# A one-core Hymba decoder step: token sums as one job ahead of the key tiles, other job times, another quarter order in the last tile, and more raw weight buffers in the gate stage

## The chip, the cores and the metric

The kernel runs on one core of one Trainium2 chip. The metric is the device time of one execution in microseconds (us), lower is better. For the kernel before, three timed runs gave a median of 2141.79 us (2141.38 to 2145.74).

The core has a matrix engine (PE, its weight loads listed as PEld), a vector engine (DVE), a scalar engine (ACT), a general engine (POOL) and an engine that mainly issues DMA transfers (SP). Each works through its own instruction stream in program order. A scheduler in the build decides that order, unless a `pin` or a `with tc.high_priority()` in the code says otherwise, and it puts in the semaphore waits.

## What is computed

The reference is one decoder layer for a prompt of 1024 tokens and 8 single-token samples with a paged cache of 4096 positions each. Width is 2048, everything is fp32.

```python
p = project(rmsnorm(xp, norm_w), w_in, b_igate, b_fgate)     # one input projection, split by columns
att = dsa_prompt(q, k, v, qi, ki, wi)    # indexer scores, top-256 positions per token, attention on those
h_ml, C1, n1, m1 = mlstm_run(mq, mk, mv, ig, lf, ...)        # mLSTM recurrence in chunks of 64
xp = merge(xp, att, p, h_ml, ml_norm_w, w_out)               # gates (az, mo, mz), output projection, residual
s = project(rmsnorm(xs, norm_w), ...)                        # the same for the 8 samples
att_s = dsa_sample(...)                  # indexer scores against the cached index keys, top 256, attention
h_s, C2, n2, m2 = mlstm_run(...)         # one recurrent step from the given state
xs = merge(xs, att_s, s, h_s, ml_norm_w, w_out)
y_prompt, y_sample = rmsnorm(xp, final_norm_w), rmsnorm(xs, final_norm_w)
```

Returned are y, the new keys, values and index keys, and the recurrent states, for the prompt and the samples.

## The kernel before

**Products.** An fp32 operand is split into a rounded part H and a remainder L, and a product is three matmuls, H·H, H·L and L·H, summed in PSUM. A weight block arrives by a DMA into a raw buffer (`wraw`); ACT rounds it into `wH` (line 251) and DVE subtracts to get `wL` (line 252). The tokens x (1032 columns: 1024 of the prompt, 8 samples) stand in SBUF as 16 rows of 128, each as xH and xL.

**Stages.** The main line of the program is PE work in six parts, by the span of the profiled run: tiles 0 to 8 of the input projection, each 128 columns wide and read in four weight quarters (misc columns, then the index queries; evacuated by DVE line 377 into `iqe`), to about 178 us; the value stage (`vproj`, lines 1559 and 1564), to 428 us; twenty tiles 17 to 36 with attention keys, values, queries and mLSTM queries and keys (line 1490), to 968 us; the gate stage (line 1717), to 1780 us; the samples' part of the output projection (line 1926), to 1882 us; the output product (line 1987), to the end.

**The gate stage** computes three gates for 24 pairs of 128 columns by a seven-product scheme of the Strassen kind: sums of weight blocks (`usD`) and sums of token blocks (`xsD`) are made beforehand in DRAM, and then 84 products (`product`) of 48 matmuls each run, with partial results added up by DVE line 1797 into buffers of a ring called `outs`. Each product takes a 128x2x512 weight block through a raw buffer, ACT line 1707 and DVE line 1708. The first two products use the tile stage's rings; from the third on there are two raw buffers, `wraw` and `wH`, and the rounded and remainder parts go into `halves`, which are the unused upper columns of the x rows 8 to 15.

**Jobs.** All else runs beside this as jobs in three lanes. A job is a generator that emits a few instructions and yields a weight; after each quarter of a tile, or at the corresponding moments of the other stages, `Lane.step` lets each lane emit as much as its job needs to be done by its `end`, counted in tiles: `T_MV` is 9 (value stage), `T_AK` 17 (first key tile), `T_MQ` 29, `T_G` 37 (gate stage), `T_PRE` 58. In the gate stage a product counts as 0.29 tiles. Lane 0 runs gates, index, att and ml; lane 1 runs prep, dscore, prep2, dsel, datt and dml; lane 2 runs usum. Those that the change touches:

- **prep** and **prep2** make the token sums for four of the eight row pairs k each. Per k: two loads X on SP (line 1386), two 1032-wide DVE operations (1391), four sums on POOL (1394 to 1397), and ten `hl` steps: an ACT rounding (1378), a DVE subtraction (1379) and an SP store to `xsD` (1380), through three buffers.
- **dscore** scores the samples against the cached index keys in 32 chunks: POOL gathers a chunk into `kp` (line 994, three buffers, two chunks ahead), PE multiplies it (line 1014).
- **usum** makes the weight sums: SP copies a block to `usD` (line 1408) and POOL adds another to it by an accumulating DMA (line 1409), 48 of these.
- **index**, **dsel** are the top-256 searches of prompt and samples (lines 489 to 566 and 1134 to 1150); **att**, **datt** the attentions; **ml**, **dml** the recurrences (ml: lines 822 to 923; dml: 1222 to 1227).

## Time and profile before

| what | value |
|---|---|
| median of three timed runs | 2141.79 us (2141.38 to 2145.74) |
| the profiled execution | 2136.99 us, of which the span of the trace is 2135.1 us |
| mean granted PE clock | 0.961 of full speed |
| DVE busy over the span | 1423.7 us (67%) |
| ACT busy | 937.4 us (44%) |
| POOL busy | 416.6 us (20%) |
| read from and written to HBM | 344.33 MB and 146.05 MB |
| work outside PE's longest groups | DVE line 494 (index scores) 95.0 us, ACT line 538 (index search) 78.5 us |

The profile is one execution. "Busy" is the time in which an engine had an instruction running. A row of the wait view names the instruction that stood idle, what it waited for, and three figures: microseconds in all, how often, and the longest. A row of the timeline gives start, duration, engine, line, operation, and in brackets the idle time ahead of it with what ended it. A row of the stretch table gives for a stretch A:B the busy time of PE, PEld, DVE, ACT and POOL with their instruction counts, the granted PE clock (1.00 is full speed), the DMA engines' busy share and GB/s.

### The profile page before, as it was taken

What the parts mean: (1) busy time and instruction counts of PE and PEld (TensorE: products, weight loads), DVE (VectorE), ACT (ScalarE), POOL (GpSimd) and SP (SyncE); (2) the same over time, 40 slices, a digit from 0 to 9 for tenths busy, and PEclk for the clock granted to TensorE, in tenths of its full rate; (3) what the DMA queues carried; (4) which work ended last, traced back from release to release, by engine and by line L of the source; (5) the groups of instructions that cost most, each with busy time, mean ns of one, the idle gap of its engine ahead of it and who ended that gap; (6) DMA issues with size and microseconds to landing.
All of it is one profiled execution on the core that took longest, in us unless ns stands there. A gap on an engine that the chain in (4) does not pass through costs nothing. (4 is left out here: it accounts for less than half of the span.)

```text
span 2135.1 us, 36131 instructions
## 1 busy us (share of the span) xinstructions
PE 1965.1 (92%) x12710; PEld 1858.0 (87%) x12710; DVE 1423.7 (67%) x3209; ACT 937.4 (44%) x1927; POOL 416.6 (20%) x420
## 2 busy tenths in 40 slices
PE   9996999999979999998769999999976988999997
PEld 9995798998879999997749999999966988987886
DVE  8445366867677677686825555555877644789887
ACT  8223345444531334531105454445764534445555
POOL 0112111213111111002320000000323632105633
PEclk9998999999989999998979999999988999999999
DMA  7575635467787685346974487538887887888875
GB/s 242 147 225 181 181 112 157 137 188 213 200 239 207 183 234 132 89 128 194 265 198 131 133 290 238 183 114 276 268 262 229 215 265 226 296 315 274 286 247 191
DMA packets 278947, 442.46 MB, mean 207 GB/s; under 512 B 40853, under 2 KB 142549, under 8 KB 274925
## 3 DMA queue, kind: packets, MB, share of 16 engines
q1 hardware_dynamic: 269533, 400.62, 59.5%
q0 software_dynamic: 7936, 37.76, 8.3%
q8 instruction: 100, 1.64, 0.3%
q10 hardware_dynamic: 1296, 1.77, 0.2%
q14 instruction: 82, 0.67, 0.1%
HBM read 344.33 MB, written 146.05 MB: 230 GB/s over the span
## 5 line engine op out<-in xcount | busy, mean ns | idle before, releaser
L1490 PE MATMUL pj<-xH,wH 128*128 128x344 f32 (+1 forms) x1200 | 390.7, 328 | 28.6 <-ACT hl L1378 12.2
L1490 PE MATMUL pj<-xL,wH 128*128 128x344 f32 (+1 forms) x1200 | 390.6, 326 | 0.0
L1490 PE MATMUL pj<-xH,wL 128*128 128x344 f32 (+1 forms) x1200 | 389.8, 326 | 0.1
L1717 PE MATMUL pj<-xH 128*128 128x258 f32 x1128 | 328.2, 291 | 32.3 <-ACT xH L1707 14.2
L1717 PE MATMUL pj<-xH,xL 128*128 128x258 f32 x1128 | 325.4, 289 | 2.4 <-DVE xL L1708 2.4
L1717 PE MATMUL pj<-xL,xH 128*128 128x258 f32 x1128 | 325.8, 289 | 0.0
L1490 PEld LDWEIGHTS pj<-xH,wH 128*128 128x128 f32 x1200 | 228.3, 191 | 32.6 <-ACT hl L1378 12.4
L1717 PEld LDWEIGHTS pj<-xH 128*128 128x128 f32 x1128 | 218.9, 194 | 36.8 <-ACT xH L1707 15.2
L1490 PEld LDWEIGHTS pj<-xL,wH 128*128 128x128 f32 x1200 | 228.2, 190 | 0.9 <-DVE xL L309 0.3
L1490 PEld LDWEIGHTS pj<-xH,wL 128*128 128x128 f32 x1200 | 228.1, 190 | 1.0 <-DVE wL L252 0.4
L1717 PEld LDWEIGHTS pj<-xH,xL 128*128 128x128 f32 x1128 | 217.9, 194 | 4.3 <-DVE xL L1708 3.9
L1717 PEld LDWEIGHTS pj<-xL,xH 128*128 128x128 f32 x1128 | 218.8, 194 | 0.7
L251 ACT CAST wH<-wraw 128x512 fp32r<-128x512 f32 (+2 forms) x187 | 112.1, 610 | 203.3 <-PE pj L1490 142.0
L252 DVE TENSOR_TENSOR wL<-wraw,wH 128x512 fp32r<-128x512 f32 (+2 forms) x187 | 133.4, 723 | 59.6 <-ACT wH L251 53.6
L1987 PE MATMUL pj<-wH,sH 128*128 128x512 f32 x336 | 132.3, 394 | 1.1 <-DVE yt L2101 0.7
L1987 PE MATMUL pj<-wH,sL 128*128 128x512 f32 x336 | 131.9, 392 | 0.0
L538 ACT ACTIVATE eq<-eq 128x512 bf16<-128x512 bf16 (+2 forms) x93 | 78.5, 844 | 118.0 <-DVE eq L537 115.8
L1987 PE MATMUL pj<-wL,sH 128*128 128x512 f32 x336 | 126.2, 394 | 3.6 <-DVE wL L1976 3.6
L491 ACT ACTIVATE rl<-bank 128x512 f32<-128x512 f32 (+2 forms) x160 | 79.0, 522 | 102.7 <-PE bank L489 83.0
L494 DVE SCALAR_TENSOR_TENSOR s<-rl,wiN,s 128x512 f32<-128x512 f32 (+2 forms) x150 | 95.0, 659 | 32.9 <-ACT rl L491 30.7
L1707 ACT CAST xH<-wraw 128x1024 fp32r<-128x1024 f32 x41 | 42.9, 1047 | 98.4 <-DMA wraw<-in_wa_dram 67.2
L1926 PE MATMUL bank<-mH,wH 128*128 128x264 f32 x256 | 74.0, 290 | 7.0 <-ACT wH L251 7.0
(507 smaller groups left out, 4769.7 us busy)
## 6 DMA issues: line engine op xcount, KB each, us to landing
wraw<-in_wt_dram SPq DMA_DIRECT2D x144, 256.0 KB
wraw<-in_wa_dram SPq DMA_DIRECT2D x114, 256.0 KB
usD<-in_wa_dram POOLq DMA_DIRECT2D x48, 512.0 KB
xsD<-hl SPq DMA_DIRECT2D x80, 258.0 KB
wraw<-in_wo_dram SPq DMA_DIRECT2D x64, 256.0 KB
usD<-in_wa_dram SPq DMA_DIRECT2D x24, 512.0 KB
usD<-usD SPq DMA_DIRECT2D x24, 512.0 KB
wraw<-usD SPq DMA_DIRECT2D x24, 512.0 KB
```

The lines of the kernel that those rows point to most:

```text
L251: a = SC.copy(H[:, s, :cols], raw[:, s, :cols])
L252: return a, V.tensor_tensor(L[:, s, :cols], raw[:, s, :cols], H[:, s, :cols].bitcast(F32), OP.subtract)
L491: SC.activation(r[:, :cn], p[:, :cn], AF.Relu)
L494: v = V.scalar_tensor_tensor(s[:, c0:c0 + cn], r[:, :cn], wv, s[:, c0:c0 + cn], OP.mult, OP.add)
L538: SC.activation(junk2[:, :W1], junk2[:, :W1], AF.Copy, accum_out=cnt[:, 1:2])
L1490: m = PE.matmul(ps[:cols, :cn], w_[:, k, :cols], x_[kk][:, c0:c0 + cn], start=(kk == 0 and z == 0), stop=(kk == 15 and z == 2))
L1707: SC.copy(H, raw)
L1717: PE.matmul(ps[c], w_[:, ks], x[y][:, c * CS:c * CS + CS], start=(first and q == 0 and k == 0 and z == 0), stop=(q == 1 and k == 3 and z = ...
L1926: PE.matmul(p, w_[:, k, :], x_, start=(n == 0), stop=(n == 47))
L1987: PE.matmul(ps[b], S_[x][:, b * 128:b * 128 + 128], T_[y], start=(k == 0 and z == 0), stop=(k == 7 and z == 2))
```

## The change

1. prep becomes one job of all eight row pairs, from tile 4 to `T_AK`; prep2 is gone. dscore, which stood between the two, now runs from `T_AK` to tile 23, and yields two steps more before its first chunk.
2. gates runs from tile 5 to `T_MV` - 0.5 and no longer in the value stage; index may emit from `T_MV` on. Ends and starts of the other jobs move: index to 34.5, att to 46.75, dsel to 33.5, datt to 38.75, ml and dml start at `T_G` + 10.25 and + 10, usum ends at `T_G` - 0.5.
3. The last tile (36) takes its weight quarters in the order 2, 3, 0, 1, so that x rows 8 to 15 are read in its first half.
4. In the gate stage all products use `halves` for the rounded and remainder parts. The first two share one raw buffer (`wraw`); from the third on a ring of four is used: two thirds of `wH`, two thirds of `wL`, a pair made of the last thirds (loaded, rounded and subtracted in two halves), and `wraw`. The two buffers for gate factors (`ones`), which stood in `wL`, go to the `rstd` space, and the ring `outs` keeps four buffers in the later phases, where it had six.

```diff
@@ job_dscore
             yield 4
             fetch(1)
             yield 4
+            yield 4
+            yield 4
             for b in range(NB):
@@ job_prep
-    def job_prep(ks):
+    def job_prep():
...
-            for k in ks:
+            for k in range(8):
@@ lanes
-    lanes = [Lane([Job("gates", T_MV, T_MV + 1.5, 8500, job_gates),
-                   Job("index", T_MV, 33, 3000 + sum(map(ix_weight, groups)), lambda: job_index(groups)),
-                   Job("att", T_MQ, 45, 2 * 2 * sum(2 * (1 + (i + 1) * 0.5) for i in range(8)) + 14, job_att, att_free),
-                   Job("ml", T_G + 8.5, T_PRE - 1, 38, job_ml)]),
-             Lane([Job("prep", 4, T_MV, 4 * 14, lambda: job_prep(range(4))),
-                   Job("dscore", T_MV, 18, 16 + 128 + 2, job_dscore),
-                   Job("prep2", T_MV, 22, 4 * 14, lambda: job_prep(range(4, 8))),
-                   Job("dsel", T_MV, 31.5, 2000 + 31 * 1700 + 10000 + 16 * 2800 + 2000, job_dsel),
-                   Job("datt", T_MQ, 37, 7500 + 8 * 5000 + 5 * 4500 + 12000 + 16000 + 5000, job_datt, ix_free),
-                   Job("dml", T_G + 8.25, T_PRE - 1.5, 28000 + 16 * 2500 + 5000, job_dml, dml_free)]),
-             Lane([Job("usum", T_AK, T_G - 0.3, 8 * NP, job_usum)])]
+    lanes = [Lane([Job("gates", 5, T_MV - 0.5, 8500, job_gates),
+                   Job("index", T_MV, 34.5, 3000 + sum(map(ix_weight, groups)), lambda: job_index(groups)),
+                   Job("att", T_MQ, 46.75, 2 * 2 * sum(2 * (1 + (i + 1) * 0.5) for i in range(8)) + 14, job_att, att_free),
+                   Job("ml", T_G + 10.25, T_PRE - 0.5, 38, job_ml)]),
+             Lane([Job("prep", 4, T_AK, 8 * 14, job_prep),
+                   Job("dscore", T_AK, 23, 24 + 128 + 2, job_dscore),
+                   Job("dsel", T_MV, 33.5, 2000 + 31 * 1700 + 10000 + 16 * 2800 + 2000, job_dsel),
+                   Job("datt", T_MQ, 38.75, 7500 + 8 * 5000 + 5 * 4500 + 12000 + 16000 + 5000, job_datt, ix_free),
+                   Job("dml", T_G + 10, T_PRE - 1, 28000 + 16 * 2500 + 5000, job_dml, dml_free)]),
+             Lane([Job("usum", T_AK, T_G - 0.5, 8 * NP, job_usum)])]
@@ mm, proj and the tile loop (mm's start and stop follow the order of the quarters)
-        for q in range(4):
+        for n, q in enumerate(qs):
...
-                lane.step(ts[0] * 4 + q)
+                lane.step(ts[0] * 4 + n)
...
-        pss = proj((t,))
+        pss = proj((t,), None, (0, 1, 2, 3) if t < T_G - 1 else (2, 3, 0, 1))
@@ gate_stage, product
-        raws, ones = [], []
+        one = wst.plain("wraw")
+        raws, ones = [[one[:, 0], one[:, 1], one]], []
...
             if turn["n"] == 3:
-                free = [wst.plain(name) for name in ("wraw", "wH", "wL")]
-                raws.extend(w[:, 0:2] for w in free[:2])
-                w = free[2].rearrange("p a b -> p (a b)")
-                ones.extend(w[:, x * HR:x * HR + HR].rearrange("p (c t) -> p c t", c=2) for x in range(2))
+                H, L = (wst.plain(name) for name in ("wH", "wL"))
+                raws[:] = [[x[:, 0], x[:, 1], x[:, 0:2]] for x in (H, L)] + [[H[:, 2], L[:, 2], None]] + raws
+                turn["raw"] = 0
             with tc.high_priority():
-                if turn["n"] < 3:
-                    hl = [wsplit(wsrc(T_G + 2 * i, q), 128, wst, 2, 3) for q in range(2)]
-                    hl = [[x.rearrange("p a b -> p (a b)") for x in y] for y in hl]
+                raw = take("raw", raws)
+                H, L = (x[turn["w"] % 4] for x in halves)
+                turn["w"] += 1
+                if raw[2] is not None:
+                    SY.dma_start(raw[2], wget(kind, i))
+                    SC.copy(H, raw[2])
+                    V.tensor_tensor(L, raw[2], H.bitcast(F32), OP.subtract)
                 else:
-                    raw = take("raw", raws)
-                    SY.dma_start(raw, wget(kind, i))
-                    H, L = (x[turn["w"] % 4] for x in halves)
-                    turn["w"] += 1
-                    SC.copy(H, raw)
-                    V.tensor_tensor(L, raw, H.bitcast(F32), OP.subtract)
-                    hl = [(H[:, q], L[:, q]) for q in range(2)]
+                    for q in range(2):
+                        SY.dma_start(raw[q], wget(kind, i)[:, q])
+                        SC.copy(H[:, q], raw[q])
+                        V.tensor_tensor(L[:, q], raw[q], H[:, q].bitcast(F32), OP.subtract)
...
-        outs += [rstd[:, c * HR:c * HR + HR].rearrange("p (c t) -> p c t", c=2) for c in range(2)]
+        ones += [rstd[:, c * HR:c * HR + HR].rearrange("p (c t) -> p c t", c=2) for c in range(2)]
```

What this does to the order of instructions is shown at three places. Each row is one instruction (or several alike, "x9") in the order of its engine: line, operation, what it writes and what it reads.

**DVE at the start of the value stage.** `L377 iqe` is the first evacuation of index tile 8, the value stage's weight remainders are `wL` of line 1555 (1556 in the changed kernel), and X and `hl` are prep's. Before:

```order
L1555 TENSOR_TENSOR wL<-wraw,wH 128x512
L1379 TENSOR_TENSOR hl<-X,hl 128x258 x2
L1555 TENSOR_TENSOR wL<-wraw,wH 128x512
L1379 TENSOR_TENSOR hl<-X,hl 128x258 x3
L1555 TENSOR_TENSOR wL<-wraw,wH 128x512
L1391 SCALAR_TENSOR_TENSOR X<-X,nw,rstd 128x1032 x2
L1379 TENSOR_TENSOR hl<-X,hl 128x258 x9
L377 TENSOR_TENSOR iqe<-pj_1628,rstd 128x388
L1379 TENSOR_TENSOR hl<-X,hl 128x258
```

With the change:

```order
L252 TENSOR_TENSOR wL<-wraw,wH 128x512
L805 COPY gT<-bank 128x96
L1556 TENSOR_TENSOR wL<-wraw,wH 128x512
L1381 TENSOR_TENSOR hl<-X,hl 128x258
L1556 TENSOR_TENSOR wL<-wraw,wH 128x512
L1381 TENSOR_TENSOR hl<-X,hl 128x258 x3
L1556 TENSOR_TENSOR wL<-wraw,wH 128x512
L1381 TENSOR_TENSOR hl<-X,hl 128x258 x2
L377 TENSOR_TENSOR iqe<-pj_1661,rstd 128x388
L392 TENSOR_TENSOR iqL<-iqe,iqH 128x388
```

Before, the pair of X operations and nine `hl` steps in a row stand right ahead of the evacuation, behind five more; with the change there is no X operation here, and six `hl` steps in all, in groups of one to three between the remainders `wL`.

**POOL in the key tiles**, from the evacuation of the value stage's or a tile's sample columns (`dec`) on. `usD` is usum's accumulating DMA, X the sums of prep2, `kp` the gather of dscore. Before:

```order
L382 COPY dec<-ev 128x8 x2
L1394 TENSOR_TENSOR X<-X 128x516
L1395 TENSOR_TENSOR X<-X 128x516
L1396 TENSOR_TENSOR X<-X 128x516
L1397 TENSOR_TENSOR X<-X 128x516
L1409 DMA usD<-in_wa_dram 64x2048 x4
L382 COPY dec<-ev 128x8
L1409 DMA usD<-in_wa_dram 64x2048 x3
L382 COPY dec<-ev 128x8
L1409 DMA usD<-in_wa_dram 64x2048 x2
```

With the change:

```order
L994 DMA kp<-in_cik_dram,idx 128x512 x2
L1411 DMA usD<-in_wa_dram 64x2048
L382 COPY dec<-ev 128x8
L994 DMA kp<-in_cik_dram,idx 128x512
L1411 DMA usD<-in_wa_dram 64x2048 x2
L994 DMA kp<-in_cik_dram,idx 128x512 x2
L1411 DMA usD<-in_wa_dram 64x2048
L994 DMA kp<-in_cik_dram,idx 128x512
L382 COPY dec<-ev 128x8
L994 DMA kp<-in_cik_dram,idx 128x512 x5
```

The sums of the row pairs are gone from here, and the gathers stand among the accumulating DMAs: from the first of the 32 gathers to the last, 12 accumulating DMAs lie between them, where there were none.

**PE in the second half of the gate stage**, where a product's matmuls (line 1717, 1718 in the changed kernel, output `pj`) meet those of ml (lines 850 to 923, output `bank`). Before, at the end of the 64th product:

```order
L1717 MATMUL pj_9376<-xH,xL 128x258
L923 MATMUL bank<-cst,hm 128x128 x4
L889 MATMUL bank<-CH,qH 128x258
L889 MATMUL bank<-CL,qH 128x258
L893 MATMUL bank<-aH,ksH 128x258
L893 MATMUL bank<-aL,ksH 128x258
L893 MATMUL bank<-aH,ksL 128x258
L889 MATMUL bank<-CH,qH 128x258
L889 MATMUL bank<-CL,qH 128x258
L893 MATMUL bank<-aH,ksH 128x258
L893 MATMUL bank<-aL,ksH 128x258
```

With the change, behind the 63rd product, at the end of the longest group of ml:

```order
L889 MATMUL bank<-aH,dH 128x258
L889 MATMUL bank<-aL,dH 128x258
L889 MATMUL bank<-aH,dL 128x258
L889 MATMUL bank<-CH,qL 128x258
L889 MATMUL bank<-aH,dH 128x258
L889 MATMUL bank<-aL,dH 128x258
L889 MATMUL bank<-aH,dL 128x258
L858 MATMUL bank<-cst,qkv 128x128 x4
L1718 MATMUL bank<-xH 128x258
L1718 MATMUL bank<-xL,xH 128x258
L1718 MATMUL bank<-xH,xL 128x258
L1718 MATMUL bank<-xH 128x258
```

Before, 108 matmuls of ml follow each other here without one of a product (the first of them are shown). With the change the longest such group in the whole stage has 30 (its last ones are shown).

More of the change, by code (lines that the diff above doesn't have):

```diff
@@ L1480, in wsrc, with mm @@
         return A["wm"][q] if t == 0 else A["wa"][t - 1 if t < T_MV else t - 9, q]
-    def mm(ps, cols, t, q, c, H, L, between={}):
+    def mm(ps, cols, t, q, c, H, L, between={}, ends=(0, 15)):
         c0, cn = chunks(t)[c]
@@ L1490, in mm, with proj @@
                 m = PE.matmul(ps[:cols, :cn], w_[:, k, :cols], x_[kk][:, c0:c0 + cn],
-                              start=(kk == 0 and z == 0), stop=(kk == 15 and z == 2))
+                              start=(kk == ends[0] and z == 0), stop=(kk == ends[1] and z == 2))
                 if k in between and z == 0:
                     pin(m)
-    def proj(ts, hook=None):
+    def proj(ts, hook=None, qs=(0, 1, 2, 3)):
         pss = []
@@ L1524, in proj @@
                     between = {(2, 0): {0: step}, (2, 1): {0: step, 2: step}}.get((x, c)) if hook and q == 3 else None
-                    mm(pss[x][c], cols, t, q, c, H, L, between or {})
+                    mm(pss[x][c], cols, t, q, c, H, L, between or {}, (qs[0] * 4, qs[3] * 4 + 3))
             for lane in lanes:
-                lane.step(ts[0] * 4 + q)
+                lane.step(ts[0] * 4 + n)
             if len(mids) > 3 or mids and not pend:
@@ L1716, in product @@
                         for z, (w_, y) in enumerate(((H, 0), (H, 1), (L, 0))):
-                            PE.matmul(ps[c], w_[:, ks], x[y][:, c * CS:c * CS + CS],
+                            PE.matmul(ps[c], w_[:, q, ks], x[y][:, c * CS:c * CS + CS],
                                       start=(first and q == 0 and k == 0 and z == 0),
@@ L1855, in gate_stage @@
                     gate(i + y, 1, 0, combine(both[y], e, OP.subtract), g)
-    lanes[1].ensure("prep2")
     lanes[2].ensure("usum")
```

1 line of the change is left out of this document (removed).

## The prediction

> **What bounds the kernel now.** I read the stretch table first, cut at the stages.
>
> ```profile
> core 0: us, PE busy (x) PEld busy (x) DVE busy (x) ACT busy (x) POOL busy (x), PEclk, DMA share, GB/s
> 178.00:428.00 250.00, 224.49 (x1174) 200.83 (x1173) 152.32 (x378) 104.16 (x240) 36.42 (x41) 0.95 0.53 153
> 428.00:968.00 540.00, 517.61 (x3229) 505.15 (x3229) 391.08 (x959) 211.59 (x431) 66.17 (x77) 0.98 0.65 181
> 968.00:1127.00 159.00, 114.88 (x765) 103.94 (x764) 89.47 (x150) 25.45 (x32) 46.21 (x43) 0.84 0.77 221
> 1127.00:1440.00 313.00, 311.80 (x2497) 306.73 (x2496) 179.91 (x477) 154.66 (x350) 0.00 (x0) 1.00 0.57 181
> 1440.00:1780.00 340.00, 294.66 (x2315) 288.52 (x2314) 224.75 (x646) 185.44 (x402) 124.44 (x142) 0.94 0.82 247
> ...
> sum 2136.00, PE 1965.13 PEld 1858.01 DVE 1423.71 ACT 937.36 POOL 416.60; mean PE 218.35 PEld 206.45 DVE 158.19 ACT 104.15 POOL 46.29
> ```
>
> PE is busy for 1965 of 2136 us, so it is the bound, and the change takes no matmul away. What can be won is PE's idle time, 171 us, and the clock lost behind idle time. The idle time is 25.5 us in the value stage, 22.4 in the key tiles, 44.1 and 45.3 at the start and in the last part of the gate stage, and 1.2 between those two, where the same products run at full clock. There 2497 matmuls took 311.8 us, 0.125 each, so a product of 48 is 6.0 us. A key tile is 540/20 = 27 us.
>
> Next I read the waits, to see what the idle time is for, and the timeline of PE for the large single gaps.
>
> ```profile
> ACT hl L1378 <- DMA xsD<-hl: 69.8, 34, 8.8
> ACT xH L1707 <- DMA wraw<-in_wa_dram: 67.2, 12, 11.7
> PE pj L1559 <- DVE iqe L377: 19.1, 1, 19.1
> ```
>
> ```profile
> 144.54 0.69 PE L1490 MATMUL pj<-xH,wH 128*128 128x388 f32 x1 [4.29 <-DVE iqe L377]
> ...
> 203.26 0.80 PE L1559 MATMUL pj<-wH,xH 128*128 128x512 f32 x1 [19.08 <-DVE iqe L377]
> ...
> 524.43 0.62 PE L1490 MATMUL pj<-xH,wH 128*128 128x344 f32 x1 [4.89 <-DVE ev L377]
> ...
> 554.40 0.40 PE L1490 MATMUL pj<-xH,wH 128*128 128x344 f32 x1 [3.66 <-DVE ev L377]
> ...
> 637.24 0.62 PE L1490 MATMUL pj<-xH,wH 128*128 128x344 f32 x1 [12.19 <-ACT hl L1378]
> ...
> 982.22 0.58 PE L1717 MATMUL pj<-xH 128*128 128x258 f32 x1 [5.26 <-ACT xH L1707]
> ...
> 1065.35 0.58 PE L1717 MATMUL pj<-xH 128*128 128x258 f32 x1 [5.66 <-ACT xH L1707]
> ```
>
> Five of the seven gaps hang on prep or prep2: an evacuation or a rounding stands in order behind `hl` steps, which wait for their stores to `xsD`. The last two are products whose weights are not there.
>
> A gap also costs clock. The stretches right behind such gaps:
>
> ```profile
> 203.30:207.60 4.30, 4.30 (x11) 3.47 (x12) 2.00 (x4) 1.27 (x3) 0.19 (x1) 0.50 0.53 158
> 207.70:212.00 4.30, 4.30 (x23) 3.83 (x22) 2.48 (x6) 3.13 (x5) 0.00 (x0) 1.00 0.63 147
> 524.50:529.00 4.50, 4.50 (x16) 4.25 (x17) 4.46 (x6) 2.03 (x6) 3.27 (x3) 0.56 1.14 363
> 637.30:642.00 4.70, 4.70 (x19) 4.70 (x20) 4.56 (x14) 1.39 (x4) 0.98 (x2) 0.60 0.83 309
> 982.30:987.00 4.70, 4.67 (x24) 4.37 (x25) 2.15 (x3) 0.00 (x0) 0.00 (x0) 0.62 0.49 112
> 1008.70:1012.00 3.30, 3.30 (x19) 3.30 (x20) 3.27 (x4) 1.50 (x3) 1.32 (x2) 0.66 0.52 184
> ```
>
> In 4.3 us at clock 0.50 PE did 11 matmuls, then 23 at 1.00: 12/23 of 4.3, or 2.2 us, were lost. By clock times length the others lost 2.0 (524.5), 1.9 (637.3) and 1.8 us (982.3).
>
> **A. Tiles 0 to 8 and the value stage (prep in one piece).** The 19.08 us consist of these rows on DVE:
>
> ```profile
> 189.13 2.50 DVE L1391 SCALAR_TENSOR_TENSOR X<-X,nw,rstd 128x1032 f32<-128x1032 f32 x2 [5.94 <-DMA X<-in_xT_dram]
> ...
> 202.65 0.56 DVE L377 TENSOR_TENSOR iqe<-pj,rstd 128x388 f32<-128x388 f32 x1
> ```
>
> 5.94 of waiting for X and 2.50 of work on it, then nine `hl` steps from 191.6 to 202.7, 1.23 us each, and only then the evacuation that PE needs. With the change, X is not ahead of it, and six `hl` steps are, spread between weight remainders. What is left of the gap lies between 0 and 6 x 1.23 = 7.4 us. I take 4, nearer to what a store's pace gives for the three or so that are not yet done when the tile ends: 15.1 won, and the 2.2 of clock stay lost. Without any gap it would be 21.3, at 7.4 left 11.7.
>
> The gap at 144 (4.29, and about 2 of clock) goes back to the same steps. Prep did 4 row pairs in 5 tile times and now does 8 in 13, 0.62 for each instead of 0.80. So it shrinks by 0 to 6.5; I take 3. Against this the value stage gets some five row pairs: 5 x (2.50 + 10 x 0.43, an `hl` step's DVE work) = 34 us of DVE, 186 of 250 us busy instead of 152, as dense as the key tiles were (391 of 540), where PE kept 96%. Those tiles' idle time outside the three named gaps was 1.7 us, so the cost is 0 to 8 (four gaps of 2); I take 3. **A: 15.1 + 3 - 3 = 15 us won**, ends 3.7 and 27.8.
>
> **B. Key tiles (prep2 gone, dscore there).** Gone are 4.89 + 3.66 + 12.19 = 20.7 of idle time and 3.9 of clock, 24.6. Two things come in. The last row pair's X operations now stand ahead of the value stage's last evacuations, the pattern of the 4.89 gap: 0 to 6.9 with clock, I take 3. And the gathers of dscore now share POOL with usum:
>
> ```profile
> POOL kp L994 <- PE bank L1014: 152.0, 19, 19.2
> ...
> POOL usD L1409 <- DMA usD<-usD: 50.3, 7, 21.4
> ```
>
> The 32 chunks have six tiles, 162 us, 5.1 us each, and a gather is issued two chunks ahead, 10.1 us. An accumulating DMA in front of it waits 50.3/7 = 7.2 us on average, which the lead hides; the longest, 21.4, would leave PE waiting 11.3. So 0 to 16 (the longest once, with smaller ones); I take 4, near the average case. PE has no row of waiting for `kp` before. **B: 24.6 - 3 - 4 = 17.6 won**, ends 1.7 and 24.6.
>
> **C. Gate start and raw buffers.** The third product waited because its load was issued only when a tile buffer came free:
>
> ```profile
> 973.86 0.46 SPq L1704 DMA_DIRECT2D wraw<-in_wa_dram  x1
> ...
> 981.12 1.04 ACT L1707 CAST xH<-wraw 128x1024 fp32r<-128x1024 f32 x1 [8.38 <-DMA wraw<-in_wa_dram]
> ...
> 1064.25 1.04 ACT L1707 CAST xH<-wraw 128x1024 fp32r<-128x1024 f32 x1 [11.66 <-DMA wraw<-in_wa_dram]
> ```
>
> From issue to rounding are 7.3 us; with the rounding (1.04) and a similar subtraction a raw buffer is held for about 9.4 us. Two buffers give 12 us, four 24: the slack grows from 2.6 to 14.6 us. The reordered tile 36 frees `halves` half a tile (13 us) early, so the first two products need no tile buffer, and the third's load has two products, 12 us, against 9.4. I count the 5.26 and 1.8 in full, and half of the gap at 1065 (5.66 and 2 of clock), since SP's order can delay a load however many buffers there are. New is that the first two products share one raw buffer: 0 to 9.4 - 6.0 = 3.4 us, I take 1. **C: 7.1 + 3.8 - 1 = 9.9 won**, ends -3.4 and 14.7.
>
> **D. ml and att later, output ring of four.** The stretch where ml runs without products:
>
> ```profile
> 1577.00:1628.00 51.00, 27.89 (x151) 25.88 (x149) 34.72 (x152) 26.39 (x70) 5.86 (x17) 0.70 0.67 206
> ...
> 1592.39 0.69 PE L923 MATMUL bank<-cst,hm 128*128 128x128 f32 x2 [7.88 <-ACT hm L915]
> ...
> 1618.45 0.69 PE L923 MATMUL bank<-cst,hm 128*128 128x128 f32 x2 [7.73 <-ACT hm L915]
> ```
>
> PE idles for 23.1 of 51 us, and at clock 0.70 its 27.9 busy us lose up to 8.4. In the new order products of 6.0 us stand between ml's groups, which would cover all but 2 of each of the two long waits: 31.5 at best, nothing if ml stalls elsewhere. I take 15, about half, as DVE is busy for 34.7 of the 51 us and has the same to do. `outs` with four buffers in place of six can delay a product's evacuation. No row before shows it; 39 partial results are loaded into that ring, and at 1 us each that is 39, at best nothing. I take 4, near nothing, because PE lost only 1.2 us from 1127 to 1440, when the ring had six and every product used it. **D: 15 - 4 = 11 won**, ends -39 and 31.5.
>
> **Sum.** 15 + 17.6 + 9.9 + 11 = 53.5. Made against the profiled execution: 2136.99 - 53.5 = 2083.5. The median of the runs stands 4.8 above that execution; I add half, as it is one draw: **2086**.
>
> [...]
>
> [...]
>
> **Rivals.** (1) *The gate stage gives its gains back* (20%): four output buffers hold up evacuations as much as C and D win. For it: DVE and POOL are busiest there. Against it: 1.2 us of idle time from 1127 to 1440. Then only A and B stay: 2136.99 + 2.4 - 32.6 = 2107.
>
> (2) *The evacuations stay behind prep* (8%): the pace of the stores is unchanged, and the gaps of A and B reappear at other tile ends and at the start of the key tiles. 2139.4 - 9.9 - 11 = 2118, up to no change if the gate stage also disappoints.
>
> (3) *Gathers behind accumulating DMAs* (8%).
>
> ```profile
> q0 software_dynamic: 7936, 37.76, 8.3%
> ```
>
> That queue held the engines for 8.3% of 2135, 177 us, for 37.76 MB, so 2.5 us for each 0.52 MB. Twelve of them lie between gathers; if each held PE up for its full length, 30 us would be lost in place of the 4 in the sum: 2112.
>
> (4) *Slower* (7%): a loop over three queues in tiles 17 to 22. POOL stands at a gather until PE has used a chunk; the accumulating DMA behind it is late; SP stands at the copy that needs it, with the tiles' weights behind. The weights are two quarters, 13.5 us, ahead. At the longest wait for PE, 19.2, each of the 12 loops costs 5.7, 68 together: 2139.4 + 68 - 53.5 = 2154. It decides from a wait of 13.5 + 53.5/12 = 18 us each; the average of the 19 waits was 8.0, which speaks against it.
>
> (5) *More than I count* (10%): the gaps of A and D go in full, 6.2 and 16.5 us more: 2063.
>
> The forecast itself has 47%, with its own range 2068 to 2104. All bad ends together would give 2176, all good ones 2041; they do not depend on each other, so the range, 2048 to 2130, takes in rivals 1, 2, 3 and 5 (2063 to 2118) and 12 to 15 us beyond them for the unknown costs. Faster by over 0.2% (4.3 us, about what a measurement of this kernel can tell from no change): 87%, that is all but rival 4 and the far end of rival 2 and of D. Within 0.2%: 5%. Slower: 8%.
>
> **What the profile of the changed kernel would show.** A: PE's wait for `iqe` at the first value matmul is under 8 us; if it is near 19, A is wrong. B: no gaps of PE over 3 us from 450 to 650 us, and no row of PE waiting for `kp`; rows of that kind with several us would speak for rivals 3 or 4. C: the wait of ACT line 1707's successor for `wraw` stays, but PE's gap behind the second product is gone. D: no 50 us in ml with PE half idle, and no PE waits for DVE's evacuations behind `ev` loads from `spD`; if there are such, rival 1 holds. My forecast is wrong if the total of PE's idle time stays above 150 us.

## The result and the profile after

The changed kernel takes 2064.11 us (median of 4 runs, 2061.64 to 2067.39) against 2141.59 us for the kernel before (4 runs). The ratio is 0.964 (95% interval 0.9614 to 0.9666), so it is 77.5 us faster. The forecast was 2086, with a range from 2048 to 2130.

The same stages in the stretch table of the changed kernel (value stage, key tiles, and the gate stage in three pieces):

```profile
core 0: us, PE busy (x) PEld busy (x) DVE busy (x) ACT busy (x) POOL busy (x), PEclk, DMA share, GB/s
179.00:393.00 214.00, 203.27 (x965) 175.49 (x963) 159.40 (x377) 109.43 (x268) 26.48 (x22) 0.98 0.66 194
393.00:946.00 553.00, 539.11 (x3427) 527.06 (x3427) 395.65 (x975) 200.25 (x394) 88.39 (x102) 0.99 0.62 174
946.00:1100.00 154.00, 129.61 (x984) 122.66 (x985) 94.43 (x166) 43.62 (x74) 38.91 (x38) 0.93 0.75 241
1100.00:1410.00 310.00, 308.08 (x2483) 303.39 (x2483) 175.32 (x465) 148.52 (x344) 1.41 (x2) 1.00 0.59 190
1410.00:1707.00 297.00, 265.19 (x2103) 259.80 (x2103) 214.68 (x619) 172.29 (x382) 123.36 (x139) 0.96 0.86 262
```

Idle time of PE fell from 25.5 to 10.7 us in the value stage, from 22.4 to 13.9 in the key tiles, and from 90.7 to 58.1 in the gate stage (before: 44.1 + 1.2 + 45.3; now 24.4 + 1.9 + 31.8). The value stage is shorter and the key tiles longer than their idle time says, because dscore's 256 matmuls moved from one to the other.

The timeline of PE at the largest gaps of the changed kernel, to be set beside the seven gaps in the prediction:

```profile
144.79 0.61 PE L1491 MATMUL pj<-xH,wH 128*128 128x388 f32 x1 [3.79 <-DVE iqe L377]
...
184.31 0.50 PE L1560 MATMUL pj<-wH,xH 128*128 128x512 f32 x1 [1.03 <-DVE iqe L377]
...
396.53 0.43 PE L1491 MATMUL pj<-xH,wH 128*128 128x344 f32 x1 [3.61 <-ACT ev L1576]
...
444.62 1.91 PE L489 MATMUL bank<-ki,qi 128*128 128x512 f32 x6 [3.99 <-DMA qi<-qS]
...
593.87 0.65 PE L1491 MATMUL pj<-xH,wH 128*128 128x344 f32 x1 [4.72 <-DVE ev L377]
...
968.81 0.58 PE L1718 MATMUL pj<-xH 128*128 128x258 f32 x1 [13.39 <-issue]
```

The 19.08 us at the start of the value stage have become 1.03, and the three gaps of the key tiles (4.89, 3.66, 12.19) have become three others of 3.6 to 4.7. The gap ahead of the third product has grown from 5.26 to 13.39. The row names "issue" as its releaser, which means that this view shows no wait. PE had run out of work at 955.42 us. The rows of the product's load on SP and of its rounding on ACT show what it waited for; the load went out 3.0 us after PE had run out, and took 9.3 us to the rounding:

```profile
958.38 1.57 SPq L1704 DMA_DIRECT2D wH<-in_wa_dram  x1
...
967.71 1.05 ACT L1705 CAST xH<-wH 128x1024 fp32r<-128x1024 f32 x1 [22.99 <-DMA wH<-in_wa_dram]
```

One table serves for all kernels below but wraw_first. Times between stage starts come from the first and last PE instruction of each stage; inside the gate stage from DVE's evacuations (lines 1797 to 1799), two for each product. The last column ends with the last evacuation, up to 6 us behind PE's last matmul, so a row adds up to a little more than the gate stage. The columns are elapsed time with the jobs' matmuls in it: a job's work that the build puts elsewhere moves time from one column to another.

| kernel (profiled execution) | value + key tiles | gate stage | products 1-12 | 13-15 | 16-24 | 25-57 | 58-63 | 64-84 |
|---|---|---|---|---|---|---|---|---|
| before | 789.1 | 811.4 | 110.0 | 56.0 | 88.1 | 298.5 | 108.6 | 151.1 |
| changed | 767.6 | 760.5 | 107.2 | 28.9 | 82.7 | 303.4 | 68.7 | 174.6 |
| prep_only | 775.9 | 791.4 | 126.7 | 20.8 | 93.9 | 295.5 | 101.9 | 153.4 |
| times_only | 799.4 | 780.8 | 110.6 | 24.7 | 80.8 | 309.9 | 91.0 | 164.5 |
| raws_back (prep + times) | 763.5 | 763.5 | 130.3 | 31.9 | 83.8 | 301.7 | 52.6 | 164.2 |
| times_back (prep + raw ring) | 780.4 | 786.5 | 109.5 | 24.0 | 82.1 | 304.7 | 103.2 | 166.2 |
| prep_back (times + raw ring) | 799.2 | 806.3 | 83.0 | 31.1 | 77.2 | 315.3 | 114.8 | 190.3 |
| late_back | 765.1 | 784.8 | 108.9 | 28.7 | 82.7 | 301.5 | 103.7 | 164.4 |
| early_back | 777.3 | 788.3 | 118.9 | 23.8 | 82.1 | 302.2 | 75.3 | 191.9 |
| outs_four | 762.6 | 774.7 | 128.3 | 31.9 | 83.8 | 301.0 | 62.1 | 169.9 |
| two_rings | 762.4 | 751.9 | 109.8 | 29.3 | 82.8 | 301.0 | 67.7 | 163.1 |
| late_gathers | 762.7 | 786.6 | 85.1 | 17.3 | 59.9 | 324.1 | 135.0 | 167.6 |
| early_sums | 765.1 | 735.4 | 95.0 | 19.2 | 85.9 | 306.8 | 67.8 | 161.6 |

The kernels raws_back, times_back and prep_back also keep the new quarter order of tile 36, which no run takes out alone.

In most rows product 63 is evacuated behind the longest group of ml in DVE's order, so the column 58-63 takes in that group. By the ends of their own matmuls products 58 to 63 take 44 to 53 us in every kernel here; the group stands on PE behind product 63 or 64. The sum of the last two columns is the safer figure.

Tiles 0 to 8 and the output projections hardly moved: the value stage starts at 178.8 us before and 178.9 now, and 355.8 and 357.4 us follow the gate stage. So the span's 70.7 us (2135.1 to 2064.4) are 21.5 from value stage and key tiles and 50.9 from the gate stage, less 1.7 elsewhere.

### The profile page after: what moved, and what is told of

The parts are those of the page before. It is cut to its first block, busy times and chain, and to the rows that moved or that the text cites. A ratio compares the mean times of both kernels' runs of the same rounds, so it can differ in the third digit from the quotient of the medians.

```text
span 2064.4 us, 36134 instructions
## 1 busy us (share of the span) xinstructions
PE 1948.8 (94%) x12710; PEld 1839.7 (89%) x12710; DVE 1426.0 (69%) x3227; ACT 934.6 (45%) x1945; POOL 421.5 (20%) x420
## 4 chain that ended last, share of the span: by engine, by line
PE 58%; DMA 16%; DVE 11%; issue 6%; ACT 4%; POOL 2%; SPq 2%; DVEq 0%; POOLq 0%; ACTq 0%
PE pj L1491 21%; PE pj L1718 11%; PE pj L1987 7%; PE bank L1926 3%; PE bank L489 2%; PE bank L634 2%; PE bank L687 2%; DMA xsD<-hl 2%; DMA gateS<-ev 2%; PE bank L1491 2%; PE bank L1718 2%; PE bank L678 1%; DMA wraw<-in_wv_dram 1%; DMA wraw<-in_wo_dram 1%; PE bank L1016 1%
## 5 line engine op out<-in xcount | busy, mean ns | idle before, releaser
L1718 PE MATMUL pj<-xH 128*128 128x258 f32 x1152 | 332.6, 289 | 34.4 <-DVE ev L1798 16.0
L1718 PE MATMUL pj<-xH,xL 128*128 128x258 f32 x1152 | 330.9, 288 | 4.5 <-DVE xL L1706 4.4
L1718 PE MATMUL pj<-xL,xH 128*128 128x258 f32 x1152 | 332.6, 289 | 0.0
L252 DVE TENSOR_TENSOR wL<-wraw,wH 128x512 fp32r<-128x512 f32 (+2 forms) x183 | 128.7, 714 | 90.9 <-ACT wH L251 80.5
L494 DVE SCALAR_TENSOR_TENSOR s<-rl,wiN,s 128x512 f32<-128x512 f32 (+2 forms) x150 | 100.1, 693 | 12.2 <-ACT rl L491 9.1
L489 PE MATMUL bank<-ki,qi 128*128 128x512 f32 (+2 forms) x320 | 79.5, 367 | 8.9 <-DMA qi<-qS 7.4
L1987 PEld LDWEIGHTS pj<-wL,sH 128*128 128x128 f32 x336 | 62.8, 188 | 22.0 <-DVE wL L1976 8.1
```

The source lines that it names most:

```text
L252: return a, V.tensor_tensor(L[:, s, :cols], raw[:, s, :cols], H[:, s, :cols].bitcast(F32), OP.subtract)
L489: PE.matmul(p[:, :cn], qi[:, h % 4, :], ki[x][:, c0:c0 + cn], start=(x == 0), stop=(x == 1))
L494: v = V.scalar_tensor_tensor(s[:, c0:c0 + cn], r[:, :cn], wv, s[:, c0:c0 + cn], OP.mult, OP.add)
L1718: PE.matmul(ps[c], w_[:, q, ks], x[y][:, c * CS:c * CS + CS], start=(first and q == 0 and k == 0 and z == 0), stop=(q == 1 and k == 3 and ...
L1987: PE.matmul(ps[b], S_[x][:, b * 128:b * 128 + 128], T_[y], start=(k == 0 and z == 0), stop=(k == 7 and z == 2))
```

## The experiments

Each kernel here is the changed kernel with an edit (some with a further one), or the kernel before with one part, and each is timed against the kernel before on its chip.

### Taking one part away

**times_back:** the job times of before.

```diff
-    Job("gates", 5, T_MV - 0.5, ...), Job("index", T_MV, 34.5, ...), Job("att", T_MQ, 46.75, ...), Job("ml", T_G + 10.25, T_PRE - 0.5, ...)
+    Job("gates", T_MV, T_MV + 1.5, ...), Job("index", T_MV, 33, ...), Job("att", T_MQ, 45, ...), Job("ml", T_G + 8.5, T_PRE - 1, ...)
     (dsel, datt, dml and usum likewise)
```

> The changed kernel with the job times of before for gates, index, att, ml, dsel, datt, dml and usum; prep in one piece, dscore in the key tiles, the quarter order and the raw ring stay. Theory 1 (the times are what takes the stalls out of the early and the late gate stage): about 33 us at the start of att and 18 us in ml come back, 2105 us (2095 to 2115), PE waits for cv and avS loads between products 12 and 15. Theory 2 (the searches end earlier because prep no longer stands in the key tiles, whatever the times): only ml's share comes back, 2082 us (2074 to 2090).

Measured: 2107.12 us, ratio 0.9843 (0.9807 to 0.9879). The total is theory 1's, the places are not. Products 13 to 15 stay short (24.0 us), and products 58 to 84 lose 26 us (269.4 against 243.3). The rest is in the key tiles, as a gap that neither the kernel before nor the changed one has:

```profile
453.35 1.19 PE L489 MATMUL bank<-ki,qi 128*128 128x512 f32 x2 [17.15 <-DMA qi<-qS]
```

PE waits for index's query block. On SP, its load is issued among usum's first copies, of which four took 8.70 us to issue (the first `qi` row below):

```profile
426.44 8.70 SPq L1410 DMA_DIRECT2D usD<-in_wa_dram  x4
435.23 0.58 SPq L471 DMA_DIRECT2D qi<-qS  x1
435.86 0.95 SPq L1410 DMA_DIRECT2D usD<-in_wa_dram  x1
436.91 0.63 SPq L248 DMA_DIRECT2D wraw<-in_wa_dram  x1
437.99 0.49 SPq L1410 DMA_DIRECT2D usD<-in_wa_dram  x1
439.44 0.36 SPq L471 DMA_DIRECT2D qi<-qS  x1
```

PE ran out only at 436.2, when that load had just been issued. By its semaphore it landed at 453.21, 18.0 us after its issue, where two others whose landing can be told took 3.8 and 5.8; the DMA engines' share over these 18 us is 0.99. So the gap is for the most part the load's time, at this share and beside these copies; what the late issue adds is not separated.

**raws_back:** the gate stage of before (two raw buffers, six output buffers).

```diff
-    def gate_stage(): ...   # ring of four raw buffers, outs of four
+    def gate_stage(): ...   # as in the kernel before
```

> The changed kernel with the gate stage of before (two raw buffers, six output buffers, the first two products from the tile rings). Theory 1 (the deeper ring pays nothing: the third product now waits 13.4 us for its load, where it waited 5.3, and this equals what later waits for raw blocks cost): 2062 us (2054 to 2070). Theory 2 (the ring is worth the 10 us of the prediction or more): 2074 us or above.

Measured: 2067.01 us, ratio 0.9656 (0.9627 to 0.9686); theory 1. The new buffers are worth 3 us, less than these intervals separate. The table shows two effects that nearly cancel: the first 12 products are 23.1 us shorter in the changed kernel (107.2 against 130.3), products 58 to 84 are 26.5 longer (243.3 against 216.8). Only part of either is waiting: PE's idle time is 24.3 against 37.6 us in the first and 31.8 against 20.4 in the second, and the rest goes with the jobs' matmuls, of which the changed kernel has 44 against 74 there and 330 against 278 here.

**prep_back:** prep, dscore and prep2 as before.

```diff
-    Job("prep", 4, T_AK, 8 * 14, job_prep), Job("dscore", T_AK, 23, 24 + 128 + 2, job_dscore),
+    Job("prep", 4, T_MV, 4 * 14, lambda: job_prep(range(4))), Job("dscore", T_MV, 18, 16 + 128 + 2, job_dscore),
+    Job("prep2", T_MV, 22, 4 * 14, lambda: job_prep(range(4, 8))),
```

> The changed kernel with prep, dscore and prep2 of before; job times, raw ring and quarter order stay. Theory 1 (moving prep pays only where it stood): the 19 us gap at the first value product and the gaps of the key tiles return, 22 us by the stage times: 2086 us (2080 to 2094). Theory 2 (prep2 also held up the searches, and with them datt and att): 22 and about 33 us come back, 2117 us (2105 to 2130).

Measured: 2147.93 us, ratio 1.0045 (1.0028 to 1.0062): 84 us above the changed kernel and slower than before. Neither theory holds. Value stage and key tiles lose 31.6 us; products 13 to 15 lose only 2; products 1 to 12 win 24; and products 58 to 84 lose 61.8 (305.1). In the program ml now has a group of 134 matmuls, and a wait that the kernel before has with 11.6 us is largest here:

```profile
DVE ev L1797 <- DMA ev<-spD: 55.0, 11, 11.7
```

DVE waits here for partial results that are still being loaded into the output ring, and PE in turn 34.1 us for these evacuations (8.9 before). The same row is in the changed kernel, with 25.2:

```profile
DVE ev L1798 <- DMA ev<-spD: 25.2, 10, 6.8
```

**wraw_first:** another order of the raw ring, aimed at the 13.39 us.

```diff
-    raws[:] = [... for x in (H, L)] + [[H[:, 2], L[:, 2], None]] + raws
+    raws[:] = raws + [... for x in (H, L)] + [[H[:, 2], L[:, 2], None]]
```

> The changed kernel with the ring of raw buffers in another order: the third product takes wraw, the fourth wH, then wL, then the pair. Theory 1 (the 13.4 us gap before the third product is its load, issued 12.7 us after the last tile's end because it stands behind that tile's stores on SP): wraw is free at once, the gap shrinks to 0 to 4 us, 2054 us (2050 to 2059). Theory 2 (the gap comes from the rounding or from the token blocks, not from the buffer): unchanged, 2064 us (2060 to 2068).

Measured: 2069.23 us, ratio 0.968 (0.9648 to 0.9713); theory 1 falls, and the time lies just above theory 2's range. The gap before the third product shrank from 13.39 to 9.73 only. The third product's load now left SP early, at 943.70, and still was not there for 18 us (the rounding's row):

```profile
961.73 1.05 ACT L1705 CAST xH<-wraw 128x1024 fp32r<-128x1024 f32 x1 [19.32 <-DMA wraw<-in_wa_dram]
```

So issuing the load 14.7 us earlier shortened the gap by 3.7 us only; the load took 18.0 us from issue to rounding, with the DMA engines' share at 1.03 from 943 to 962 us. The stretch table of the changed kernel there:

```profile
945.00:955.00 10.00, 9.15 (x75) 8.89 (x74) 2.68 (x5) 0.00 (x0) 7.89 (x8) 1.00 1.02 299
955.00:965.00 10.00, 0.42 (x4) 0.21 (x2) 6.42 (x7) 0.00 (x0) 2.02 (x2) 0.78 1.04 321
965.00:975.00 10.00, 6.10 (x29) 5.80 (x30) 9.90 (x11) 3.24 (x4) 3.04 (x3) 0.53 1.04 371
...
985.00:1000.00 15.00, 9.17 (x54) 8.76 (x54) 14.79 (x16) 2.19 (x3) 6.28 (x7) 0.77 1.03 391
```

and of the kernel before:

```profile
965.00:975.00 10.00, 10.00 (x81) 9.81 (x80) 9.96 (x20) 1.24 (x2) 1.76 (x1) 1.00 0.49 154
975.00:985.00 10.00, 4.70 (x28) 4.20 (x27) 8.04 (x13) 1.04 (x1) 0.00 (x0) 0.70 0.44 137
985.00:1000.00 15.00, 12.68 (x88) 12.31 (x88) 5.87 (x24) 3.27 (x4) 8.17 (x7) 0.86 0.65 154
```

The column before the last is the DMA engines' busy share. It was 0.44 to 0.65 at the start of the gate stage; now it is 1.01 to 1.04 from 945 to 1000 us. datt, which the earlier search lets start sooner (its key gathers run from 943 to 996 us, before from 990 to 1044), has its loads and gathers here, beside usum's last copies, the token sums and the weights of the next products.

### One part alone

**prep_only** and **times_only**, the kernel before with one of these parts.

```diff
 prep_only: the kernel before
-    Job("prep", 4, T_MV, 4 * 14, ...), Job("dscore", T_MV, 18, 16 + 128 + 2, ...), Job("prep2", T_MV, 22, 4 * 14, ...)
+    Job("prep", 4, T_AK, 8 * 14, job_prep), Job("dscore", T_AK, 23, 24 + 128 + 2, job_dscore)
 times_only: the kernel before
-    Job("gates", T_MV, T_MV + 1.5, ...), Job("index", T_MV, 33, ...), Job("att", T_MQ, 45, ...), ...
+    Job("gates", 5, T_MV - 0.5, ...), Job("index", T_MV, 34.5, ...), Job("att", T_MQ, 46.75, ...), ...
```

> The kernel before with prep in one piece and dscore in the key tiles, and nothing else of the change. Theory 1 (the parts add up where the runs so far say: without prep the rest is worth nothing, so prep alone is worth what times_back shows): 2110 us (2102 to 2118), with the long group of ml still in the gate stage. Theory 2 (prep is worth the 84 us that prep_back lost): 2057 us.

> The kernel before with the changed job times, and nothing else of the change. Theory 1 (later times pay only when prep is out of the key tiles): 2145 us (2137 to 2153), no better than before. Theory 2 (the times are worth the 43 us that times_back lost, wherever prep stands): 2098 us (2090 to 2106).

Measured: prep_only 2107.73 us, ratio 0.9856 (0.9825 to 0.9887); times_only 2115.19, ratio 0.9894 (0.9863 to 0.9925). prep_only is theory 1's, times_only lies between its two theories, outside both ranges and nearer to theory 2 (17 us above it, 30 below theory 1). Against the kernel before timed beside them (2138.9) the two are worth 31 and 24 us, and both together with the new quarter order (raws_back, 2067.01 against 2140.71) 74. Either alone takes the stall of products 13 to 15 away (56.0 to 20.8 and 24.7), so that gain counts once. prep_only pays for it with the 17 us gap for index's query block (17.6 us here), which the changed times of gates, index, dsel, datt and usum remove (early_back, below). And only both together bring products 58 to 84 down to 216.8 us (255.3 and 255.5 with one part).

**late_back** and **early_back** split the job times.

```diff
 late_back: the changed kernel
-    Job("att", T_MQ, 46.75, ...), Job("ml", T_G + 10.25, T_PRE - 0.5, ...), Job("dml", T_G + 10, T_PRE - 1, ...)
+    Job("att", T_MQ, 45, ...), Job("ml", T_G + 8.5, T_PRE - 1, ...), Job("dml", T_G + 8.25, T_PRE - 1.5, ...)
 early_back: the changed kernel
-    Job("gates", 5, T_MV - 0.5, ...), Job("index", T_MV, 34.5, ...), Job("dsel", T_MV, 33.5, ...), Job("datt", T_MQ, 38.75, ...), Job("usum", T_AK, T_G - 0.5, ...)
+    Job("gates", T_MV, T_MV + 1.5, ...), Job("index", T_MV, 33, ...), Job("dsel", T_MV, 31.5, ...), Job("datt", T_MQ, 37, ...), Job("usum", T_AK, T_G - 0.3, ...)
```

> The changed kernel with the times of before for att, ml and dml alone. Theory 1 (these times decide how ml is interleaved with the products; PE's order then has a group of 86 ml matmuls where the changed kernel's longest has 30): about 26 us more from product 58 on, as in times_back, 2090 us (2082 to 2098). Theory 2 (the length of the groups does not matter, since DVE bounds ml): 2064 us (2058 to 2070).

> The changed kernel with the times of before for gates, index, dsel, datt and usum alone; att, ml and dml stay late. Theory 1 (the earlier gates and the later ends of the searches carry the 17 us of the 43 that are not ml's, 13 of them in the key tiles): 2081 us (2074 to 2088), with PE waiting for the index job's query load before tile 19 for over 10 us, as in times_back (17.2). Theory 2 (the late times carry all 43): 2064 us (2058 to 2070).

Measured: late_back 2085.34 us, ratio 0.9759 (0.9728 to 0.9791); early_back 2099.72, ratio 0.9812 (0.978 to 0.9844). late_back is theory 1's: products 58 to 63 lose 35.0 us and 64 to 84 win 10.2. As said above, the 35.0 is the group counted into that column; the two columns together lose 24.8. PE's rows in the long group of ml:

```profile
1526.05 0.69 PE L923 MATMUL bank<-cst,hm 128*128 128x128 f32 x2 [10.19 <-ACT hm L915]
...
1553.30 0.69 PE L923 MATMUL bank<-cst,hm 128*128 128x128 f32 x2 [8.51 <-ACT hm L915]
```

early_back's gap for the query block is there as expected:

```profile
451.47 0.76 PE L489 MATMUL bank<-ki,qi 128*128 128x512 f32 x1 [18.45 <-DMA qi<-qS]
```

but the total, 36 us above the changed kernel, is over theory 1's 17: products 1 to 12 lose 11.7 and 64 to 84 lose 17.3 more, which I had not counted. Its longest group of ml is about as short as in the changed kernel (32 matmuls of jobs on PE in both), and still products 58 to 84 lose 23.9, as much as in late_back: here PE waits 29.5 us for DVE's evacuations, up to 10.0 at once (16.0 and 3.8 in the changed kernel). The two halves (21 and 36) are together more than the whole (43).

### The buffers of the gate stage, and what beats the change

**outs_four** and **two_rings** separate the raw ring from the output ring.

```diff
 outs_four: raws_back
-        outs += [rstd[:, c * HR:c * HR + HR].rearrange("p (c t) -> p c t", c=2) for c in range(2)]
 two_rings: the changed kernel
-        ones += [rstd[:, c * HR:c * HR + HR].rearrange("p (c t) -> p c t", c=2) for c in range(2)]
+        outs += [rstd[:, c * HR:c * HR + HR].rearrange("p (c t) -> p c t", c=2) for c in range(2)]
...
         fill(0, 4)      # after product 48
+        w = wL3[0].rearrange("p a b -> p (a b)")      # wL3 holds the whole of wL; the lines that set it are left out
+        ones.extend(w[:, x * HR:x * HR + HR].rearrange("p (c t) -> p c t", c=2) for x in range(2))
+        raws[:] = [raws[0], raws[3]]
+        turn["raw"] = 0
```

> raws_back (the changed kernel with the gate stage of before) with four output buffers in the later phases where it has six; the raw buffers stay two. Theory 1 (the ring of raw buffers wins some 25 us in the first 24 products and the missing two output buffers lose as much behind product 57): the 24 first products as in raws_back, products 58 to 84 about 25 us longer, 2092 us (2084 to 2100). Theory 2 (the late loss comes from the order of ml that the scheduler happens to choose, or from the deeper raw ring's traffic): 2067 us (2061 to 2073).

> The changed kernel with the raw ring of four for the first 48 products, and from then on the buffers of before: two raw buffers, the factor buffers in wL, and the rstd space as fifth and sixth output buffer (these two from product 25 on). Theory 1: it keeps the early gain and loses no output buffer, 2040 us (2032 to 2050), products 58 to 84 about 25 us shorter than in the changed kernel. Theory 2 (two raw buffers late cost as much as six outputs win): 2064 us (2057 to 2071).

Measured: outs_four 2075.0 us, ratio 0.9716 (0.9691 to 0.9741); two_rings 2058.12, ratio 0.9625 (0.9598 to 0.9652). The direction is theory 1's in both, the size a third and a quarter of it: outs_four lies outside both ranges, and two_rings inside theory 2's. Taking two output buffers away costs 8 us; behind product 57 it is 15.2 (232.0 against 216.8), and other stretches give some back. The wait for partial results in the ring goes from 11.6 us (raws_back, 2.5 at `ev` and 9.1 at `rstd`, which is part of its ring of six) to 38.1:

```profile
DVE ev L1798 <- DMA ev<-spD: 38.1, 11, 10.8
```

Giving them back late, with the raw ring kept early, wins 6 us on the changed kernel (the intervals overlap, and by the ratios it is 3), and the view of two_rings has 1.8 us of this wait. The rest of raws_back's 26.5 us stayed when the buffers were given back (230.8 against 216.8). The order of ml differs there, with a longest group of 30 against none over 22; what else does, these runs do not separate.

**late_gathers** and **early_sums**, both on two_rings, ask what fills the DMA engines at the start of the gate stage.

```diff
 late_gathers: two_rings
-    Job("datt", T_MQ, 38.75, ...)
+    Job("datt", T_G + 1.25, 40, ...)
 early_sums: two_rings
-    Job("usum", T_AK, T_G - 0.5, 8 * NP, job_usum)
+    Job("usum", T_AK, T_G - 3, 8 * NP, job_usum)
```

> two_rings with datt (the samples' attention, whose gathers of cached keys and values are large DMAs) starting at T_G + 1.25 and ending at tile 40, in place of T_MQ and 38.75. Theory 1 (the 13 us gap before the third product is DMA traffic: datt's gathers and query loads, which now fall together with the first product loads, so that the DMA engines are full from 945 to 1000 us): the gap before the third product is under 5 us and the first 12 products take 95 us or less (110 in two_rings). Theory 2 (the place of the load on SP): gap and 110 us stay. In either case PE's order now has a group of 186 ml matmuls, where two_rings has 30: if such groups cost what late_back showed, products 58 to 84 take 280 us or more (231 in two_rings), and the whole is 2085 to 2105 us; if not, 2045 to 2060.

> two_rings with usum ending at T_G - 3 in place of T_G - 0.5, so that its last copies and accumulating DMAs lie in the key tiles and not at the start of the gate stage. Theory 1 (any of the DMA traffic there delays the product loads): the first 12 products take about 100 us (110 in two_rings), 2050 us (2044 to 2056). Theory 2 (datt's gathers alone are enough to fill the engines): no change, 2058 us (2053 to 2063).

Measured: late_gathers 2090.56 us, ratio 0.9796 (0.9756 to 0.9836); early_sums 2037.62, ratio 0.954 (0.9503 to 0.9577). With datt later, the first 12 products take 85.1 us (24.7 less), but the gap before the third product stays, at 12.1 (12.6 in two_rings). Part of the 24.7 is no gain: datt's own 44 matmuls, 15.5 us of PE, went elsewhere with it. PE's idle time there fell from 26.6 to 12.7, so datt costs the later of these products and not this gap; whether by its gathers or by its work on DVE, the run does not separate. With a group of 186 ml matmuls products 58 to 84 take 302.6 us, 71.8 more, and the total is in the range expected for that. early_sums goes theory 1's way, further than its range. With usum earlier, the gap before the third product shrinks to 5 us, the first 12 products take 95.0 and the next three 19.2:

```profile
956.95 0.58 PE L1719 MATMUL pj<-xH 128*128 128x258 f32 x1 [4.95 <-ACT xH L1706]
```

The DMA engines' share is still 0.98 to 1.04 from 945 to 985 us there, but at 985 to 1000 it is down to 0.52, where two_rings has 0.91:

```profile
955.00:965.00 10.00, 8.02 (x41) 7.72 (x42) 8.09 (x10) 3.23 (x4) 2.62 (x2) 0.66 1.04 376
...
985.00:1000.00 15.00, 14.96 (x124) 14.78 (x125) 14.86 (x18) 5.08 (x8) 3.64 (x4) 1.00 0.52 155
```

early_sums is faster than the changed kernel, 0.954 against 0.964 with intervals that do not meet, and some 100 us faster than the kernel before.

## Why the prediction was right in direction and 22 us short

**A. Start of the value stage: right, and somewhat better.** Of the 19.08 us, 1.03 are left where the sum kept 4. The 2.2 us of clock that the sum gave up were won too: the granted clock is 1.00 from 184.3 to 188.0 us. The gap at 144 us did not shrink as assumed (3.79 of 4.29), so 0.5 was won there where 3 were counted. Idle time in the whole value stage is down by 14.8; outside the one gap it rose from 6.4 to 9.7, close to the 3 that were put down for a denser DVE. But 1.35 and 2.05 us of it are waits of PE for index's query block, and not for DVE.

**B. Key tiles: the gaps went, but only about half of the sum came.** Idle time went down by 8.5 us where 13.7 were counted (20.7 less 3 and 4), and the 3.9 of clock are not seen: PE's busy time in the two stages together is 742 us before and now. A and B together won 21.5 us of time where the sum had 32.6. The pattern at the start of the key tiles came as priced (3.61 against 3): DVE waits 4.38 us for X and works on it, ACT's rounding waits for that, and the evacuation that PE needs stands behind it:

```profile
393.72 2.50 DVE L1393 SCALAR_TENSOR_TENSOR X<-X,nw,rstd 128x1032 f32<-128x1032 f32 x2 [4.38 <-DMA X<-in_xT_dram]
...
395.05 0.72 ACT L1380 CAST hl<-X 128x258 fp32r<-128x258 f32 x2 [4.53 <-DVE X L1393]
395.67 0.80 ACT L1576 ACTIVATE ev<-pj,rtok 128x256 f32<-128x256 f32 x2
```

The gathers cost nothing: the changed kernel has no row of PE waiting for `kp`. In times_back and early_back PE waits once each for a gather, 1.9 and 1.7 us. Not foreseen were two gaps, 3.99 for index's query block and 4.72 for an evacuation at 594, which stands on DVE behind a step of the search that waits 8.59 us for its own store (`biasS`). The first is what is left of something the prediction did not see at all: moving prep creates a gap of 17 to 18 us there (times_back, prep_only, early_back), and the changed times of gates, index, dsel, datt and usum, which the prediction gave no price, take most of it away. Which of these five does it was not tried.

**C. Raw buffers: wrong.** The step "I count the 5.26 and 1.8 in full" failed: the gap became 13.39. The sum let the third product's load go out two products, 12 us, ahead and take 7.3 us. In the changed kernel it left SP at 958.38, 11.8 us after the first product began, behind the stores of tile 36 and a wait of 3.1 us for datt's query loads, and took 9.3. Nor would an earlier place on SP have saved the step: issued 14.7 us sooner in wraw_first, the load took 18 us. Over the 7.3 us of the load in the kernel before the DMA engines' share was 0.76, over these 9.3 and these 18 it was 1.03. Even so the deeper ring made the first 12 products 23 us shorter than two buffers in the same place (raws_back), 13 of them in idle time of PE, because two buffers then fare worse still (one gap of 16 us). Together with the output ring the buffers are worth 3 us where C and the ring's 4 came to 6.

**D. ml and the output ring: right mechanism, right size for the sum of the two.** Products 58 to 84 won 16.4 us (259.7 to 243.3) where 11 (15 less 4) were counted. The wait that the prediction wanted to cover with products, PE's for `hm`, is less than half of what it was. It is 7.9 to 14.3 us where the longest group of ml has 30 matmuls or fewer (changed, raws_back, two_rings), and 21.9 to 40.0 where it has 86 or more, though not in step with its length. These rows are of the kernel before (108 matmuls in the group), the changed kernel (30), late_back (86) and prep_back (134):

```profile
PE bank L923 <- ACT hm L915: 21.9, 6, 7.9
PE bank L923 <- ACT hm L915: 7.9, 3, 5.0
PE bank L923 <- ACT hm L915: 32.7, 6, 10.2
PE bank L923 <- ACT hm L915: 38.5, 7, 10.5
```

In late_gathers (186) the figure is 40.0. The group is not all: early_back has a short one, an `hm` wait of 13.9, and loses as much at the evacuations. The output ring was put at 4 us; outs_four measures 8 in all, and 15 behind product 57. That term was misread twice: the wait view of before does have the row "DVE ev L1797 <- DMA ev<-spD", with 11.6 us, and the 39 partial results are only those at `ev`; 21 more go to the two buffers at `rstd`. The waits for `ev` that the prediction named as a sign of its first rival are there (25.2 us), and PE's for the evacuations rose from 8.9 to 16.0 us. PE's idle time in all is 115.6 us (2064.4 less 1948.8), well under the 150 that would have spoken against the forecast.

**What the sum lacked: products 13 to 15.** They took 56.0 us before and take 28.9 now, 27 us that no step of the sum had; 22 of them are idle time of PE. The gaps were in the profile of before:

```profile
1098.54 1.06 PE L1349 MATMUL bank<-cv,PZ 128*32 128x256 f32 x2 [6.87 <-DMA cv<-in_cv_dram,ixv]
...
1103.93 1.06 PE L1349 MATMUL bank<-cv,PZ 128*32 128x256 f32 x2 [2.84 <-DMA cv<-in_cv_dram,ixv]
...
1119.45 0.88 PE L597 MATMUL bank<-cst,pP 128*128 128x128 f32 x3 [5.70 <-DMA pP<-avS]
```

They are datt's values and att's first loads. The prediction priced "ml and att later" by ml alone. With the searches done earlier, one gap of 1.76 for `cv` is left. prep_only and times_only each take this stall away. In prep_only the samples' search ends 41 us sooner (its store `slotS` leaves SP at 940 us, before at 981), and datt's value gathers begin at 1000 in place of 1044. In times_only that store leaves at 979 and the gathers begin at 1037, only 2 and 7 us sooner; what removes the stall there is not shown. From profiled execution to profiled execution the change is worth 70.9 us (2136.99 to 2066.14) where the sum had 53.5: 27.1 more here, 11.1 less in A and B, 2.9 more in the rest of the gate stage, 1.6 less in the output projections and outside the span. The medians add 6.6, since the profiled execution lay 4.6 below the median before and 2.0 above it now.

Without the gain in products 13 to 15 the time would have been about 2091, 5 us from the forecast. That closeness is in part luck: 11 us are missing in A and B, and what C and D and the medians gave beyond the sum stands against them. The rivals: the first (gate stage gives back) is what happened to the buffers, not to the stage. Of the second, the gap at 144 us and the 3.61 are what came. The third and fourth (gathers, the loop over three queues) did not come. The fifth (more than I count) names almost the measured time, 2063, but by gaps of A and D that go in full; what came instead is the stall of products 13 to 15.

**Open.** The length of ml's groups is set by the build's scheduler, and the runs show what it costs but not why moving prep shortens it (134 in prep_back, 30 in the changed kernel, none over 22 in raws_back). The raw ring alone on the kernel before and the quarter order of tile 36 alone were not tried. The two parts are not additive, and why both together win 74 us where 31 and 24 were won alone is known only in part: either takes the stall of products 13 to 15, and the changed times take the gap that prep creates.

## What to carry to other kernels

A change that moves background work forward also moves the DMAs behind it; look at what those land on, and take load times for the new place from a stretch with as full a DMA (here the 7.3 us at a share of 0.76 became 9.3 and 18 at 1.03). Parts of such a change are not additive: two of them removed the same stall, and one created an 18 us stall that the other removed, so try them alone and together. Where two rings share a space, split by phase who needs it: raw buffers early and output buffers late, with the DRAM copies finished ahead of the stage, beat the change by 1.0% of the time before, 21 us (26 by the medians, on two chips).
